# Six projection steps behind each GELU, stores on ScalarE's queue, and operand buffers of the out stage opened at the last projection

## The chip, the cores and the metric

One core of a Trainium2 chip. The metric is the device time in microseconds of one execution. TensorE, VectorE, ScalarE, GpSimd and SyncE stand in the profile as PE, DVE, ACT, POOL and SP; SP and a part of POOL only issue transfers here. Each engine takes its instructions in the order of its own list.

## The reference

One layer over x (2048 x 1024), all in float32: one input projection, eight heads of forgetting attention beside spatial gating on eight groups, a common out projection, then a SwiGLU FFN.

```python
xn = rms_norm(x, mix_norm_g)
q, k, v, f_logit, z = split(xn @ w_in)          # 512, 512, 512, 8, 1024
attn = forgetting_attention(q, k, v, log_sigmoid(f_logit + b_f))
zu, zv = split(gelu(z))                          # exact GELU, 512 each
zv = layer_norm(zv, ln_g, ln_b)
sgu = zu * (einsum('gij,bcjgd->bcigd', masked w_s, zv) + b_s)
merged = concat(rms_norm(attn), rms_norm(sgu))
x = x + merged @ w_out
x = x + (silu(gate) * up) @ w_down               # gate, up from rms_norm(x) @ w_gate_up
return rms_norm(x, final_norm_g)
```

## The kernel before

Matrix products are made of split operands: each float32 operand is rounded to a high part (a cast on ACT, L110) and a low part (the rest, a subtraction on DVE, L113), and high by high, high by low and low by high are summed, so a product is three matmuls. The program runs in four stages: the projection of q, k and v (to 341 us), the attention stage with the z projection and the gating worked in between (to some 1010 us), the out projection (its matmuls, `oz`, L1072, from 928.8 us on), and the FFN (L1509).

The attention stage is a loop of 320 steps (h, j, kb): head, chunk of 512 queries, block of 128 keys. In a step `qk` makes two score matmuls `st` (L674, L675), an exp on ACT (L677, `Pt`), a cast `Ph` (L110, ACT) and the low part `Pl` (L113, DVE). `pv_of` multiplies both by V two steps later (L707, L709, L712). There are two `st` banks. A stream `lm` makes the row maxima ahead (L332 on PE, L334 on DVE). At the end of a (h, j), `fin` copies the row sums (`lv`, L720, ACT), stores one row of them to SD (L721, SP), makes the numerator `nd` (L722) and stores it to AT (L723, SP). When a chunk has all heads, the sums are read back, inverted and stored to RD (L728 to L731).

Into these steps the generator `gates()` weaves the z projection: 256 projection steps of three matmuls (L824), paced by the step number over ZEND = 280 of the 320 steps. `z_proj` takes a group of four 128-token tiles, with operands `xz` loaded by SP; behind its 32 steps stands one GELU over the whole group (L832). There are eight groups, so eight GELUs: four of the v half, each followed by `v_side` (layer norm, mixing), then four of the u half, each followed by `u_side`: product with the mixed gate (L881), squares (L883), scaling (L888), PE transposes (L891), copies `wsth`/`wstl` on ACT (L894) and a store to ST (L895, SP).

The out stage takes per 128-token tile the transposed operands from ST and AT (`out_prep`, L989, L990), multiplies by RD (L993, L997), squares and sums (L1001 to L1015), and splits. At step OPEN = 268 the preparation of tiles 0 and 1 starts in the gating's own buffers. After the last projection and the gating's end, `stz.close()` frees the gating's buffers, and `out_open()` opens the out stage's: `strm` (raw operands and their high and low parts), `xap`, `pev` and the PSUM pool. From the next step on `out_tiles` puts out matmuls between the last attention steps, for tiles 0 and 1 first.

`behind(*newest)` orders an instruction after the newest cast and low part of the attention, so that it does not overtake them. The order of an engine's list otherwise comes from a scheduler that works on what the program states.

Of the kernel before, what the change touches and what calls it, by code (L numbers as in the profile page):

```python
# [58 lines left out]
LEND = 276  # L59
LEAD = 14  # L60
ZF = 3
OPEN = 268
ORATE = 2
FT = 9
ND = 4
# [12 lines left out]
def trunk(ctx: ExitStack, tc: tile.TileContext, x, x_t, mix_g, w_in, b_f, ln_g, ln_b, w_st, b_st, on_g, w_out,  # L78
# [505 lines left out]
    ps2_[0] = ps2  # L584
    stz = st2.enter_context(ExitStack())
    p2z = pool(stz, "p2z", bufs=2)
    p2m = pool(stz, "p2m", bufs=2)
    psz = pool(stz, "psz", bufs=2, space=PSUM)
    wst_h = T(p2z, [P, 8, P], F32R, "wsth", bufs=1)
    wst_l = T(p2z, [P, 8, P], F32R, "wstl", bufs=1)  # L590
# [125 lines left out]
    def fin(h, j):  # L716
        pr, o = h // 2, (h % 2) * DH
        pv, _ = live.pop((h, j))
        nd, lv = T(p2, [DH, CH], F32, "nd", bufs=1), T(p2, [DH, CH], F32, "lv", bufs=1)
        nc.scalar.copy(lv, pv[DH:P])  # L720
        ld(SD[j][h : h + 1], lv[0:1])  # L721
        nc.vector.scalar_tensor_tensor(nd, lv, m0[0:DH], pv[0:DH], ALU.mult, ALU.add)  # L722
        ld(AT[j][o : o + DH, pr, :], nd)  # L723
        heads[j] += 1
        if heads[j] == H:
            yield
            sr = T(p2, [P, H * CH // P], F32, "sr")
            ld(sr, SD[j].rearrange("h (a t) -> (h a) t", t=H * CH // P))  # L728
            yield
            nc.vector.reciprocal(sr, sr)  # L730
            ld(RD[j].rearrange("h (a t) -> (h a) t", t=H * CH // P), sr)  # L731
        yield
# [3 lines left out]
    def z_consts():  # L736
        wsr = T(p2z, [P, 8, P], F32, "zr", bufs=2)
        yield
        ld(wsr, w_st.rearrange("g j i -> j g i"))
        bsc = T(p2z, [P, 8], F32, "bsc", bufs=1)  # L740
        ld(bsc, b_st)
        lngb = T(p2z, [P, 512], F32, "lngb", bufs=1)
        ld(lngb, ln_g.rearrange("(o n) -> o n", o=1).broadcast_to([P, 512]))
        lnbb = T(p2z, [P, 512], F32, "lnbb", bufs=1)
        ld(lnbb, ln_b.rearrange("(o n) -> o n", o=1).broadcast_to([P, 512]))
        ZC.update(bsc=bsc, lngb=lngb, lnbb=lnbb)
        yield
        nc.vector.memset(wsr[64:128, :, 0:64], 0.0)
        hi_of(nc.scalar, wst_h, wsr)
        lo_of(nc.vector, wst_l, wsr, wst_h)  # L750
        yield
# [45 lines left out]
    def at_u(*at):  # L797
        if at == (0, 2, 0):
            ld(onc, on_g.rearrange("(k p) -> p k", p=P))
            wl_[:] = out_part(0)  # L800
            wl_[0](0, raw2)
            wl_[0](1, raw2)
        if at in O_AT:
            n = O_AT.index(at)
            wl_[1](n)
            if n in (1, 3):
                wl_[0](n // 2 + 2, raw2)
        if at[1:] == (3, 4):
            m = mixes[at[0]] = T(p2z, [P, 4, CH], F32, "zvh", bufs=1)
            ld(m, GD[at[0]])  # L810

    def z_proj(q, w, side, extra):

        zr = T(p2z, [P, 4, CH], F32, "zr", bufs=2)
        for cc in range(4):
            t = 4 * q + cc
            xz = T(p2z, [P, 2, KT, P], F32R, "xz")
            for a in range(2):
                ldr(xz[:, a], XS[q][:, a, :, cc * P : (cc + 1) * P])
            pz = T(psz, [P, CH], F32, "z", bufs=NZ)  # L820
            n = 0
            for k in range(KT):
                for a, b in ((0, 0), (0, 1), (1, 0)):
                    nc.tensor.matmul(pz, xz[:, a, k, :], w[b][:, k, :], start=n == 0, stop=n == 3 * KT - 1)  # L824
                    n += 1
                extra(q, cc, k)
                if k % 2:
                    next(side, None)
                yield
            nc.scalar.activation(zr[:, cc, :], pz, AF.Copy, scale=r1[:, t : t + 1])  # L830
        with behind(*newest):
            nc.scalar.activation(zr, zr, AF.Gelu)  # L832
        return zr

    def v_side(q, zr):

        yield
        yield
        mv = T(p2, [P, 4, 2], F32, "mv", bufs=1)
        for cc in range(4):  # L840
            with behind(*newest):
                bs = T(p2, [P, 6], F32, "bs")
                nc.vector.bn_stats(bs, zr[:, cc, :])
                nc.vector.bn_aggr(mv[:, cc, :], bs)
            if cc % 2:
                yield
        rv = rsqrt(p2, mv[:, :, 1], 1.0, "rl", n=4)
        zvh = T(p2z, [P, 8, 4, DH], F32R, "zvh", bufs=1)
        zvl = T(p2z, [P, 8, 4, DH], F32R, "zvl", bufs=1)
        for cc in range(4):  # L850
            with behind(*newest):
                zv = zr[:, cc, :]
                nc.vector.scalar_tensor_tensor(zv, zv, mv[:, cc, 0:1], ZC["lngb"], ALU.subtract, ALU.mult)
                nc.vector.scalar_tensor_tensor(zv, zv, rv[:, cc : cc + 1], ZC["lnbb"], ALU.mult, ALU.add)
                zv8 = zv.rearrange("p (g d) -> p g d", g=8)
                hi_of(nc.scalar, zvh[:, :, cc, :], zv8)
                lo_of(nc.vector, zvl[:, :, cc, :], zv8, zvh[:, :, cc, :])
            yield
        for gg in range(4):
            px = T(psz, [P, 2, 4, DH], F32, "z", bufs=NZ)  # L860
            for g2 in range(2):
                g = gg * 2 + g2
                for n, (a, b) in enumerate(((wst_h, zvh), (wst_h, zvl), (wst_l, zvh))):
                    nc.tensor.matmul(px[:, g2].rearrange("p c d -> p (c d)"), a[:, g, :],
                                     b[:, g].rearrange("p c d -> p (c d)"), start=n == 0, stop=n == 2)
            yield
            for g2 in range(2):
                g = gg * 2 + g2
                nc.vector.tensor_scalar_add(zr[:, :, g * DH : (g + 1) * DH], px[:, g2], ZC["bsc"][:, g : g + 1])
        ld(GD[q], zr)  # L870
        yield

    def u_side(q, zr):

        yield
        yield
        ss = T(p2, [P, 4], F32, "ss2", bufs=1)
        m = mixes.pop(q)
        for cc in range(4):
            with behind(*newest):  # L880
                nc.vector.tensor_tensor(zr[:, cc, :], zr[:, cc, :], m[:, cc, :], ALU.mult)  # L881
                jk = T(p2, [P, CH], F32, "jk", bufs=1)
                nc.scalar.activation(jk, zr[:, cc, :], AF.Square, accum_out=ss[:, cc : cc + 1])  # L883
            yield
        rs = rsqrt(p2, ss, 1.0 / 512, "rs", n=4)
        yield
        for cc in range(4):
            nc.vector.tensor_scalar_mul(zr[:, cc, :], zr[:, cc, :], rs[:, cc : cc + 1])  # L888
            tp = T(psz, [P, 4, P], F32, "z", bufs=NZ)
            for k in range(4):  # L890
                nc.tensor.transpose(tp[:, k, :], zr[:, cc, k * P : (k + 1) * P], ident)  # L891
            yield
            sT = T(p2z, [P, 4, P], F32, ("wsth", "wstl")[cc % 2], bufs=1)
            nc.scalar.copy(sT, tp)  # L894
            ld(ST[4 * q + cc], sT)  # L895


    units = [(h, j) for h in range(H) for j in range(NCH)]
# [2 lines left out]
    def gates():  # L901
        side = iter(())
        for w, extra, then in ((wzv, at_v, v_side), (wzu, at_u, u_side)):
            for q in range(NCH):
                zr = yield from z_proj(q, w, side, extra)
                for _ in side:
                    yield "on"
                side = then(q, zr)
        for _ in side:
            yield  # L910
# [57 lines left out]
            yield  # L968

    def out_open():  # L970
        nonlocal strm, pev, xap
        xap = pool(ctx, "xap", bufs=2, side="right")
        strm = pool(ctx, "strm", side="right")
        pev = evac_pool(0)
        pso = pool(ost, "pso", bufs=2, space=PSUM)
        E["bank"] = lambda: T(pso, [P, CH], F32, "oz")
# [5 lines left out]
    def out_prep(t, o, space=None):  # L982
# [40 lines left out]
        if space is not None:  # L1023
            o["ahead"] = True
            while not strm:
                yield
            inputs()
            low = split(r[:, 4:8, :])
        o["s"] = (split(at), low)
        yield  # L1030

# [74 lines left out]
    zc = z_consts()  # L1106
    next(zc)
    zg = gates()
    z_total = H * 4 * KT
    z_done = o_done = 0  # L1110
    og = wg = None
    fins = []
# [2 lines left out]
    for n in range(len(steps) + DEPTH):  # L1115
# [25 lines left out]
        if z_done == z_total and not wg:  # L1141
            while next(zg) == "on":
                pass
            wg = out_weights()
        if n >= OPEN:
            if not first:
                E["tp"] = lambda: T(ps2, [P, 4, P], F32, "mx_ps", bufs=NMX)
                z = T(p2z, [P, 4, 4, P], F32, "zvl", bufs=1)
                first += [out_prep(t, o[t], (z[:, 2 * t], z[:, 2 * t + 1])) for t in range(2)]
            with behind(*newest):  # L1150
                for g in first:
                    next(g, None)
        if z_done == z_total and not strm:
            if all([next(zg, 0) == 0 for _ in range(ZF)]) and all(o[t].get("ahead") for t in range(2)):
                stz.close()
                out_open()
                o_from = n + 1
        if strm and not og and n > o_from:
            og = out_tiles()
        while og and o_done < (n - o_from) * ORATE:  # L1160
            with behind(*newest):
# [409 lines left out]
```

## Time and profile before

| | us |
|---|---|
| median of 3 runs | 2455.67 |
| lowest, highest | 2453.19, 2455.75 |
| the profiled execution | 2457.9 |
| its span, first to last instruction | 2456.2 |
| PE busy in it | 2386.1 (97%) |
| DVE, ACT, POOL busy | 1664.5, 1054.6, 611.1 |
| mean granted TensorE clock | 0.985 of full |

The shares are means over four stages with different limits. A stretch in which PE stands still, or in which its granted clock is below 1, is found in the table by stretches and in the timelines; a gap of a line is the idle time ahead of it on its own engine, with what ended it.

### The profile page before, as it was taken

To read this page: it belongs to the slowest core of one execution; us is meant where nothing else is said; L and a number is where in the kernel's file an instruction comes from. 1 tells how busy PE (TensorE), PEld (TensorE's weight loads), DVE (VectorE), ACT (ScalarE), POOL (GpSimd) and SP (SyncE) were. 2 spreads that over 40 slices of the span, in tenths; PEclk is the share of its full clock that TensorE was granted. 3 is DMA by queue.
4 is the path that set the end of the run, shared out by engine and by line. 5 is a ranking of instruction groups with operands and counts; after the bars stand their busy time and mean duration, and the time that the engine had idled before them with its cause. 6 is when DMAs were issued, how large, how long until landed. Compare 5 with 4: busy or idle time off the path is not lost. (4 is left out here: it accounts for less than half of the span.)

```text
span 2456.2 us, 31368 instructions
## 1 busy us (share of the span) xinstructions
PE 2386.1 (97%) x10585; PEld 1903.9 (78%) x10585; DVE 1664.5 (68%) x2710; ACT 1054.6 (43%) x1770; POOL 611.1 (25%) x662
## 2 busy tenths in 40 slices
PE   9999999999999988999999999999999999999997
PEld 7778777777777666778888888888888887888886
DVE  6557667888877555555765555875555587696888
ACT  5322137766777664434432323433233242332333
POOL 1000011122111211122232322233223244454441
PEclk9999999999999989999999999999999999999999
DMA  8856466555565656665523223342222335455453
GB/s 283 285 168 202 132 198 180 157 153 164 150 179 160 167 155 196 189 193 170 172 77 103 69 86 86 107 134 69 86 80 84 95 114 187 172 189 192 148 186 144
DMA packets 404919, 372.08 MB, mean 151 GB/s; under 512 B 72660, under 2 KB 326420, under 8 KB 402712
## 3 DMA queue, kind: packets, MB, share of 16 engines
q1 hardware_dynamic: 401880, 359.59, 47.7%
q0 software_dynamic: 2880, 10.49, 1.4%
q8 instruction: 85, 1.39, 0.2%
q14 instruction: 74, 0.61, 0.1%
HBM read 249.09 MB, written 120.92 MB: 151 GB/s over the span
## 5 line engine op out<-in xcount | busy, mean ns | idle before, releaser
L110 ACT CAST wh<-raw 128x512 fp32r<-128x512 f32 (+2 forms) x496 | 304.1, 620 | 756.4 <-PE pp L1509 609.9
L113 DVE TENSOR_TENSOR wl<-raw,wh 128x512 fp32r<-128x512 f32 (+2 forms) x496 | 370.9, 757 | 93.5 <-ACT wh L110 93.2
L1509 PE MATMUL pp<-wl,wh 128*128 128x512 f32 x1056 | 326.5, 390 | 1.7 <-ACT u L1265 1.0
L1509 PE MATMUL pp<-wh,wh 128*128 128x512 f32 x1056 | 326.1, 390 | 0.0
L1199 POOL TENSOR_TENSOR raw<-raw 128x512 f32<-128x512 f32 (+1 forms) x124 | 170.4, 1375 | 507.1 <-DMA raw<-in_w_gu_dram 342.8
L113 DVE TENSOR_TENSOR Pl<-Pt,Ph 128x512 fp32r<-128x512 f32 (+1 forms) x320 | 194.9, 613 | 109.1 <-ACT Ph L110 96.7
L1509 PEld LDWEIGHTS pp<-wl,wh 128*128 128x128 f32 x1056 | 198.0, 188 | 44.7 <-ACT u L1265 1.4
L1509 PEld LDWEIGHTS pp<-wh,wh 128*128 128x128 f32 x1056 | 198.2, 188 | 41.9
L677 ACT ACTIVATE Pt<-st 128x512 f32<-128x512 f32 (+1 forms) x320 | 167.3, 533 | 129.8 <-PE st L675 125.5
L1509 PE MATMUL pp<-wl,wl 128*128 128x512 f32 x528 | 206.2, 391 | 0.7 <-DVE wl L113 0.7
L1509 PE MATMUL pp<-wh,wl 128*128 128x512 f32 x528 | 206.0, 390 | 0.0
L824 PE MATMUL z<-wh,xz 128*128 128x512 f32 x512 | 191.8, 403 | 2.1 <-DMA xz<-XS 2.1
L1199 DVE TENSOR_TENSOR raw<-raw,raw 128x512 f32<-128x512 f32 (+1 forms) x112 | 133.3, 1192 | 79.0 <-POOL raw L1199 75.2
L110 ACT CAST Ph<-Pt 128x512 fp32r<-128x512 f32 (+1 forms) x320 | 175.3, 557 | 26.4 <-PE pv L709 11.3
L334 DVE TENSOR_REDUCE mx<-mx_ps 128x1 f32<-128x512 f32 x192 | 129.4, 684 | 35.5 <-PE mx_ps L332 35.1
L687 POOL TENSOR_SCALAR_AFFINE_SELECT Ph<-Ph 128x128 fp32r<-128x128 f32 x128 | 49.4, 386 | 409.6 <-DVE Pl L113 317.0
L674 PE MATMUL st<-A,D 74*128 74x512 f32 (+1 forms) x320 | 123.9, 387 | 9.2 <-ACT Pt L677 8.9
L707 PE MATMUL pv<-Ph,V 128*128 128x512 f32 (+1 forms) x320 | 122.4, 382 | 10.5 <-POOL Ph L687 6.1
L712 PE MATMUL pv<-Pl,V 128*128 128x512 f32 (+1 forms) x320 | 123.3, 385 | 1.8 <-DVE Pl L113 1.0
L332 PE MATMUL mx_ps<-D,A 66*128 66x512 f32 (+2 forms) x320 | 118.2, 385 | 6.0 <-DMA D<-KH 3.7
L675 PE MATMUL st<-B,C 128*128 128x512 f32 (+1 forms) x320 | 120.4, 376 | 0.0
L1509 PEld LDWEIGHTS pp<-wl,wl 128*128 128x128 f32 x528 | 99.1, 188 | 23.0 <-DVE wl L113 1.6
(315 smaller groups left out, 5300.6 us busy)
## 6 DMA issues: line engine op xcount, KB each, us to landing
raw<-in_w_gu_dram SPq DMA_DIRECT2D x88, 512.0 KB
xz<-XS SPq DMA_DIRECT2D x64, 512.0 KB
HD<-hT SPq DMA_DIRECT2D x44, 512.0 KB
D<-KH SPq DMA_DIRECT2D x112, 128.0 KB
XA<-xa SPq DMA_DIRECT2D x27, 512.0 KB
raw<-HD SPq DMA_DIRECT2D x24, 512.0 KB
XA<-xb SPq DMA_DIRECT2D x21, 512.0 KB
xa<-XA SPq DMA_DIRECT2D x20, 512.0 KB
```

The lines of the kernel that those rows point to most:

```text
L110: return nc.scalar.copy(o, i) if eng is nc.scalar else eng.tensor_copy(o, i)
L113: return eng.tensor_tensor(o, i, f(h), ALU.subtract)
L332: nc.tensor.matmul(pm[:, 0:n], lhs, Dt[0 : lhs.shape[0], 0:n], start=True, stop=True)
L334: nc.vector.tensor_reduce(mx[:, a, s : s + 1], pm, AX.X, ALU.max)
L674: nc.tensor.matmul(st[:, off:], Dt[:, b * P : (b + 1) * P], A[:, off:], start=True, stop=False)
L675: nc.tensor.matmul(st[:, off:], C[:, b * P : (b + 1) * P], B[:, off:], start=False, stop=True)
L677: nc.scalar.activation(Pt[:, off:], st[:, off:], AF.Exp)
L707: nc.tensor.matmul(pv[:, off:], V[:, 0:P], Ph[:, off:], start=kb == 0, stop=False)
L712: nc.tensor.matmul(pv[:, off:], V[:, 0:P], Pl[:, off:], start=False, stop=kb == 4 * j + 3)
L824: nc.tensor.matmul(pz, xz[:, a, k, :], w[b][:, k, :], start=n == 0, stop=n == 3 * KT - 1)
L1199: (nc.vector if e == "v" else nc.gpsimd).tensor_tensor(o, a, b, op)
L1509: nc.tensor.matmul(pm, a[:, k, :], b[:, k, :], start=on is None and k == 0 and e == 0, stop=k == it.kh - 1 and e == 2, skip_group_check=n ...
```

## The change

It has three parts. First, `z_proj` gets a number `burst`: for the first six projection steps of a group it yields "on", which makes the loop go on at once, so with the step that follows seven projection steps stand in a row at the beginning of a group, that is behind the GELU of the group before. The first group has none. The pace of the others is spread over 42 steps fewer. Second, the stores of row sums to SD and of transposed tiles to ST are issued by ACT. Third, some of the gating's buffers (`lngb`, `lnbb`, `xz`, `zvl` and those of the row maxima) lie in a pool set `sty` of their own, which is closed at the last projection; `strm` takes its place there, so the second half of w_out and the low parts of tiles 0 and 1 are made before the gating has ended. The row maxima and the preparation of tiles 0 and 1 are driven to their ends at that point. `stz.close()` and `out_open()` wait for the gating alone. OPEN becomes 265, and from the second group of u on the mixed gate is loaded at another step.

```diff
-OPEN = 268
+OPEN = 265
+BURST = 6
...
-    p2m = pool(stz, "p2m", bufs=2)
+    sty = st2.enter_context(ExitStack())
+    p2y = pool(sty, "p2y", bufs=2)
+    p2m = pool(sty, "p2m", bufs=2)
...
-        ld(SD[j][h : h + 1], lv[0:1])
+        nc.scalar.dma_start(SD[j][h : h + 1], lv[0:1])
...
-        if at[1:] == (3, 4):
+        if at[1:] == ((2, 0) if at[0] else (3, 4)):
             m = mixes[at[0]] = T(p2z, [P, 4, CH], F32, "zvh", bufs=1)
             ld(m, GD[at[0]])
...
-    def z_proj(q, w, side, extra):
+    def z_proj(q, w, side, extra, burst):
...
-                yield
+                yield "on" if cc == 0 and k < burst else None
...
-            ld(ST[4 * q + cc], sT)
+            nc.scalar.dma_start(ST[4 * q + cc], sT)
...
-                zr = yield from z_proj(q, w, side, extra)
+                zr = yield from z_proj(q, w, side, extra, 0 if q == 0 and then is v_side else BURST)
...
     def out_open():
-        nonlocal strm, pev, xap
+        nonlocal pev, xap
         xap = pool(ctx, "xap", bufs=2, side="right")
-        strm = pool(ctx, "strm", side="right")
...
             while not strm:
                 yield
+            low = split(r[:, 4:8, :])
+            o["s"] = (split(at), low)
+            while not xap:
+                yield
             inputs()
-            low = split(r[:, 4:8, :])
+            yield
+            return
...
-    z_total = H * 4 * KT
+    z_total = H * 4 * KT - 7 * BURST
...
         if z_done == z_total and not wg:
             while next(zg) == "on":
                 pass
+            for _ in lm:
+                pass
+            while not all(o[t].get("ahead") for t in range(2)):
+                for g in first:
+                    next(g)
+            sty.close()
+            strm = pool(ctx, "strm", side="right")
             wg = out_weights()
...
-        if z_done == z_total and not strm:
-            if all([next(zg, 0) == 0 for _ in range(ZF)]) and all(o[t].get("ahead") for t in range(2)):
+        if wg and not xap:
+            if all([next(zg, 0) == 0 for _ in range(ZF)]):
                 stz.close()
                 out_open()
                 o_from = n + 1
-        if strm and not og and n > o_from:
+        if xap and not og and n > o_from:
             og = out_tiles()
```

PE at the sixth GELU (755.1 us in the trace), before, from the score pair on whose exp is the first behind the GELU; line numbers and tile numbers differ a little between the two programs:

```order
L674 MATMUL st_8363<-A_8070,D_858_3356 128x512
L675 MATMUL st_8363<-B_8073,C_853_3351 128x512
L707 MATMUL pv_8181<-Ph_8314,V_847_3338 128x256
L709 MATMUL pv_8181<-Ph_8314,V_847_3338 1x256
L712 MATMUL pv_8181<-Pl_8316,V_847_3338 128x256
L674 MATMUL st_8380<-A_8070,D_858_3356 128x512
L675 MATMUL st_8380<-B_8073,C_853_3351 128x512
L332 MATMUL mx_ps_8389<-D_8109,A_7620 128x512
L707 MATMUL pv_8181<-Ph_8332,V_847_3338 128x128
L709 MATMUL pv_8181<-Ph_8332,V_847_3338 1x128
L712 MATMUL pv_8181<-Pl_8334,V_847_3338 128x128
L674 MATMUL st_8399<-A_8070,D_858_3356 128x512
```

The same place in the changed program, from the score pair whose exp is the last ahead of the GELU:

```order
L677 MATMUL st_8356<-A_8078,D_858_3359 128x512
L678 MATMUL st_8356<-B_8081,C_853_3354 128x512
L827 MATMUL z_8373<-wh_3233,xz_8370 128x512
L827 MATMUL z_8373<-wl_3234,xz_8370 128x512
L827 MATMUL z_8373<-wh_3233,xz_8370 128x512 x2
L827 MATMUL z_8373<-wl_3234,xz_8370 128x512
L827 MATMUL z_8373<-wh_3233,xz_8370 128x512 x2
L827 MATMUL z_8373<-wl_3234,xz_8370 128x512
```

Before, PE has one more score pair and small PV matmuls there. Now the projection of the next group follows, 21 matmuls in a row, of which the first are shown.

ACT at the eighth GELU, before:

```order
L830 ACTIVATE zr_9160<-z_9764,r_2_64 128x512
L677 ACTIVATE Pt_10128<-st_10125 128x512
L832 ACT_TABLE_LOAD
L832 ACTIVATE zr_9160<-zr_9160 128x2048
L110 CAST Ph_10130<-Pt_10128 128x512
L677 ACT_TABLE_LOAD
L677 ACTIVATE Pt_10155<-st_10152 128x512
L883 ACTIVATE jk_9926,ss_2673_9924<-zr_9160 128x512
```

And now, with what each instruction waits for (`DMAHW0` to `DMAHW7` are the eight landing semaphores that transfers of SP and ACT take in turn; the other names are engines):

```order
L723 COPY lv_9903<-pv_9606 64x512 [waits DMAHW1_49,PE_49]
L680 ACTIVATE Pt_9892<-st_9889 128x512 [waits PE_49]
L724 DMA SD_110_173<-lv_9903 1x512 [waits DMAHW0_49,Activation_49]
L111 CAST Ph_9894<-Pt_9892 128x512 [waits Activation_49,Pool_49]
L680 ACTIVATE Pt_9913<-st_9910 128x512 [waits DVE_49,PE_49]
L833 ACTIVATE zr_9163<-z_9748,r_2_64 128x512 [waits PE_49]
L111 CAST Ph_9915<-Pt_9913 128x512 [waits DVE_49,Activation_49]
L835 ACT_TABLE_LOAD
L835 ACTIVATE zr_9163<-zr_9163 128x2048 [waits Activation_49]
L111 CAST wh_9932<-raw_9637 128x512 [waits DMAHW3_49,DMAHW2_49]
L111 CAST wh_9936<-raw_9637 128x512 [waits DMAHW7_49,DMAHW1_49]
L111 CAST wh_9940<-raw_9642 128x512
```

Now a store to SD stands between an exp and a cast, and waits for a landing semaphore too; casts of the out operands (`wh<-raw`) follow the GELU, four in all, ahead of the next exp.

SP at the opening of the out stage, before (`raw_10112` is the operand tile of token tile 2):

```order
L895 DMA ST_98_161<-wsth_10010 128x512
L107 DMA V_848_3339<-VD_77_140 128x4x1
L895 DMA ST_99_162<-wstl_10019 128x512
L107 DMA C_856_3354<-KH_3_58_121 64x512
L107 DMA C_856_3354<-KL_3_74_137 64x512
L721 DMA SD_111_174<-lv_10339 1x512
L978 DMA ffb_10049<-in_ffn_g_dram 128x1024
L989 DMA raw_2727_10099<-ST_87_150 128x512
L990 DMA raw_2727_10099<-AT_100_163 128x4x128
L993 DMA rd_10100<-RD_112_175 64x4x128 x2
L989 DMA raw_10112<-ST_86_149 128x512
L990 DMA raw_10112<-AT_100_163 128x4x128
```

And now, where that tile is `raw_10128`:

```order
L991 DMA raw_2732_10128<-ST_86_149 128x512
L992 DMA raw_2732_10128<-AT_100_163 128x4x128
L108 DMA C_856_3357<-KL_3_74_137 64x512
L108 DMA D_861_3362<-AUG_146 10x4x128
L991 DMA raw_2823_10500<-ST_88_151 128x512
L992 DMA raw_2823_10500<-AT_101_164 128x4x128
L980 DMA ffb_10079<-in_ffn_g_dram 128x1024
L1010 DMA xa_10096<-in_x_dram 128x1024
L1010 DMA xa_10098<-in_x_dram 128x1024
L995 DMA rd_10116<-RD_112_175 64x4x128 x2
L995 DMA rd_10129<-RD_112_175 64x4x128 x2
```

The loads of tile 2 stood behind two of the last four stores to ST, a store to SD and the loads of tile 3; now no store is ahead of them here, and the loads of x and RD come behind.

## Rows read from the trace of the kernel before

**Rows 1.** The page, busy time, share of the span and instructions of each engine.

```profile
PE 2386.1 (97%) x10585; PEld 1903.9 (78%) x10585; DVE 1664.5 (68%) x2710; ACT 1054.6 (43%) x1770; POOL 611.1 (25%) x662
```

**Rows 2.** Stretches: from:to, length, PE, PEld, DVE, ACT, POOL busy (instructions), clock, DMA share, GB/s.

```profile
480.00:490.00 10.00, 10.00 (x44) 7.38 (x43) 6.83 (x12) 9.87 (x14) 0.00 (x0) 1.00 0.38 96
...
555.00:558.40 3.40, 3.18 (x8) 2.30 (x9) 1.27 (x3) 3.37 (x6) 0.00 (x0) 0.50 0.27 93
...
691.50:698.30 6.80, 6.20 (x15) 4.85 (x16) 3.22 (x5) 3.17 (x6) 0.00 (x0) 0.50 0.61 149
...
759.80:766.60 6.80, 6.35 (x15) 4.85 (x16) 4.80 (x8) 4.73 (x9) 0.00 (x0) 0.50 0.19 43
...
831.50:834.90 3.40, 3.40 (x10) 1.98 (x11) 2.18 (x4) 3.35 (x8) 0.54 (x2) 0.50 1.00 279
...
910.00:920.20 10.20, 8.36 (x27) 5.32 (x25) 6.66 (x14) 7.84 (x19) 2.66 (x7) 0.50 0.00 0
...
944.10:954.40 10.30, 5.18 (x14) 4.08 (x15) 8.08 (x14) 2.66 (x5) 2.23 (x3) 0.50 0.61 159
440.00:480.00 40.00, 39.13 (x192) 30.94 (x191) 33.62 (x67) 26.15 (x49) 7.87 (x16) 1.00 0.63 177
```

**Rows 3.** Timeline of ACT at the sixth GELU: start, duration, engine, line, operation.

```profile
755.08 1.28 ACT L832 ACT_TABLE_LOAD   x1
756.38 1.91 ACT L832 ACTIVATE zr<-zr 128x2048 f32<-128x2048 f32 x1
758.30 1.28 ACT L677 ACT_TABLE_LOAD   x1
```

**Rows 4.** Timeline of PE at the sixth GELU; in brackets idle time before, and its releaser.

```profile
755.77 0.40 PE L674 MATMUL st<-A,D 74*128 74x512 f32 x1
756.01 0.40 PE L675 MATMUL st<-B,C 128*128 128x512 f32 x1
...
760.25 0.80 PE L674 MATMUL st<-A,D 74*128 74x512 f32 x1 [3.38 <-ACT Pt L677]
760.84 0.63 PE L675 MATMUL st<-B,C 128*128 128x512 f32 x1
761.26 0.63 PE L674 MATMUL st<-A,D 74*128 74x512 f32 x1
```

**Rows 5.** Timelines of PE at the third, fifth and seventh GELU.

```profile
555.22 0.80 PE L707 MATMUL pv<-Ph,V 128*128 128x512 f32 x1 [0.58 <-ACT Ph L110]
...
692.10 0.80 PE L674 MATMUL st<-A,D 74*128 74x512 f32 x1 [1.79 <-ACT Pt L677]
...
828.65 1.10 PE L332 MATMUL mx_ps<-D,A 66*128 66x512 f32 x2 [0.55 <-DVE mx L334]
831.38 0.61 PE L674 MATMUL st<-A,D 74*128 74x384 f32 x1 [1.63 <-ACT Pt L677]
```

**Rows 6.** Timeline of PE behind the eighth GELU.

```profile
909.55 0.50 PE L707 MATMUL pv<-Ph,V 128*128 128x512 f32 x1 [3.14 <-DMA D<-KH]
...
911.46 0.69 PE L674 MATMUL st<-A,D 74*128 74x384 f32 x1 [0.61 <-ACT Pt L677]
...
915.89 0.79 PE L707 MATMUL pv<-Ph,V 128*128 128x512 f32 x1 [1.22 <-POOL Ph L687]
```

**Rows 7.** Timelines of PE and ACT at the opening of the out stage.

```profile
949.22 0.58 PE L1015 MATMUL mx_ps<-ones_c,sq 128*128 128x1 f32 x2 [8.85 <-POOL sq L1004]
...
943.66 0.62 ACT L110 CAST wh<-raw 128x512 fp32r<-128x512 f32 x1 [9.70 <-DMA raw<-ST]
```

**Rows 8.** SP's waits (total, times, longest), ST stores (ns min/median/max), landing of POOL's loads (us).

```profile
SPq L721 <- ACT lv L720: 41.8, 18, 7.6
SPq L107 <- DVE mr L351: 34.7, 9, 9.1
...
L895 SPq DMA_DIRECT2D ST<-wsth x8: 319/332/1633, 726.7 to 923.4; - x8
...
raw<-in_w_out_dram POOLq DMA_DIRECT2D x6, 512.0 KB, 5.3
```

More of the change, by code (lines that the diff above doesn't have):

```diff
@@ L741, in z_consts @@
         ld(bsc, b_st)
-        lngb = T(p2z, [P, 512], F32, "lngb", bufs=1)
+        lngb = T(p2y, [P, 512], F32, "lngb", bufs=1)
         ld(lngb, ln_g.rearrange("(o n) -> o n", o=1).broadcast_to([P, 512]))
-        lnbb = T(p2z, [P, 512], F32, "lnbb", bufs=1)
+        lnbb = T(p2y, [P, 512], F32, "lnbb", bufs=1)
         ld(lnbb, ln_b.rearrange("(o n) -> o n", o=1).broadcast_to([P, 512]))
@@ L816, in z_proj @@
             t = 4 * q + cc
-            xz = T(p2z, [P, 2, KT, P], F32R, "xz")
+            xz = T(p2y, [P, 2, KT, P], F32R, "xz")
             for a in range(2):
@@ L848, in v_side @@
         zvh = T(p2z, [P, 8, 4, DH], F32R, "zvh", bufs=1)
-        zvl = T(p2z, [P, 8, 4, DH], F32R, "zvl", bufs=1)
+        zvl = T(p2y, [P, 8, 4, DH], F32R, "zvl", bufs=1)
         for cc in range(4):
@@ L1147, in trunk @@
                 E["tp"] = lambda: T(ps2, [P, 4, P], F32, "mx_ps", bufs=NMX)
-                z = T(p2z, [P, 4, 4, P], F32, "zvl", bufs=1)
+                z = T(p2y, [P, 4, 4, P], F32, "zvl", bufs=1)
                 first += [out_prep(t, o[t], (z[:, 2 * t], z[:, 2 * t + 1])) for t in range(2)]
```

## The prediction

> **What bounds the kernel now.** I read the page first: TensorE is busy 2386.1 of 2456.2 us [rows 1], so time can come only from the places where it stands still or runs at half clock. The table by stretches of the attention stage [rows 2] shows where: most stretches look like 440 to 480 us, with PE busy 39.13 of 40 us at full clock and VectorE 33.62, but there are short stretches at a granted clock of 0.50, the lower level of 1.2 GHz. Four of them stand right behind GELUs (the third, fifth, sixth and seventh of eight), one behind the eighth, and one at the opening of the out stage. The timelines tell why. ScalarE's GELU is 1.28 + 1.91 + 1.28 us of table load, activation and table load back [rows 3], and no exp is made in these 4.5 us. PE works off what it has behind the last score pair, then waits for the next exp: 3.38 us at the sixth GELU [rows 4], 0.58, 1.79 and 0.55 + 1.63 us at the third, fifth and seventh [rows 5]. At the second nothing is lost, as the stretch from 480 to 490 us shows [rows 2]; the first and the fourth are alike.
>
> **The bursts.** The idle time at these four GELUs is 0.58 + 1.79 + 3.38 + 2.18 = 7.9 us. Behind each the clock falls: 3.4, 6.8, 6.8 and 3.4 us at 0.50 [rows 2]. Full matmuls start 0.42 us apart there, against 0.24 us just before [rows 4], so about half of such a stretch is lost: 20.4 / 2 = 10.2 us. Together 18.1 us, the most that the bursts can give back at GELUs 1 to 7. Seven projection steps are 21 matmuls, 21 x 0.24 = 5.0 us of PE work that waits for no exp. At the sixth GELU PE lacked 3.4 us; the order puts 21 of them in a row behind the last score pair, and at the other six places it is the same kind of row. The work is only moved: 42 steps fewer are spread between the GELUs, 42 x 3 x 0.24 = 30 us over some 560 us. VectorE, busy 84% there [rows 2], then has up to 5% less time per attention step, which it still has. I take **-17 us**, a little under the whole, since exps may come late in other places; the ends are 0 and -18.1.
>
> The Trainium skill (ScalarE: Activation LUTs, section What ACT_TABLE_LOAD costs) speaks against this cover: it puts a switch of tables at about 2.66 us, a load of some 1.28 us and a drain of some 1.38 us. By that a GELU would hold the exps up about 7.2 us (an estimate from that page), 2.8 more, and a burst would leave gaps at the GELUs that have little else behind them. In the trace the activation starts 1.30 us after the load, and the load back 1.92 us after the activation [rows 3]: no drain shows, and the sum goes by the rows.
>
> **The eighth GELU** has no burst. PE idles 3.14 + 0.61 + 1.22 us there [rows 6], and 10.2 us are at half clock [rows 2]. In the new order four casts of out operands and one square stand between GELU and the load back, where one cast stood: about four more ScalarE instructions of the size of the cast at 943.66 us, 0.62 us [rows 7], so 2.5 us. PE has about 2 us more behind its last score pair than before, counted from its rows at 0.24 us a full matmul. Ends: 0 and +2.5 for the wait, and up to half of a further 3.4 us at low clock. I take **+3 us**.
>
> **The opening of the out stage.** PE stands 8.85 us at the sum of squares of token tile 2 and then runs 949.2 to 954.4 us at half clock, 5.2 / 2 = 2.6 us: 11.4 us [rows 7, 2]. ScalarE had waited 9.70 us for the load from ST [rows 7], so the chain is load, product, square, two GpSimd adds, PE, behind 48 out matmuls that PE does in a row with nothing else. In the new order of SyncE these loads stand ahead of the x tiles and the RD loads, no longer behind ST and SD stores, and score and PV matmuls stand between the out matmuls. The chain, some 9 us, then runs under that work. I take **-10 us**, most of 11.4; ends 0 (the chain is as late again, since RD of this chunk or ScalarE is late) and -11.4.
>
> **The stores on ScalarE's queue.** 32 stores of row sums and 16 of transposed tiles leave SyncE and go between exps. The issue itself was 0.33 us for an ST store on SyncE [rows 8]; 48 x 0.33 = 16 us of ScalarE time, in a stage where it is busy 26.15 of 40 us [rows 2]: nothing on the path. What the stores may wait for costs more. Each DMA takes one of eight landing semaphores in turn, and 46 of the 48 wait until the transfer that had it before, mostly one of SyncE's eight places back, has landed. ScalarE is in order, so the casts and exps behind a store wait as well, then the score matmuls. The trace of before has no such wait. Lower end: all those transfers have long landed, 0. Upper end for one store: the transfer's own landing, 5.3 us for 512 KB in the nearest row, or that SyncE has not issued it yet since it stands in a wait itself, up to 9.1 us for VectorE [rows 8]. SyncE waits a good part of this stage, and I estimate that a third of the stores, 15, find such a transfer open, for 2.5 us on average, 38 us of ScalarE. What that costs PE is read from the GELUs: eight times 4.5 us without an exp gave 7.9 + 5.0 = 12.9 us idle, a share of 0.36, but a short stall stays under PE's stock of work more often. I take half of 0.36 x 38: **+6 us**. On the other side SyncE no longer stands 41.8 us in 18 waits for the row-sum copies [rows 8], so its key loads come earlier; PE hardly waited for them, and I give nothing for it.
>
> **The rest.** The preparation of tiles 0 and 1 is driven to its end in one piece at the last projection, with its SD store, row-sum load, reciprocal, RD store and loads, while projection operands stand behind it on SyncE: 0 to +8 (about the chain of 8.85 us of tile 2, without its cover); I take **+3 us**. The second half of w_out loads earlier on GpSimd's queue and costs nothing new. The load of the mixed gate at step (2,0) instead of (3,4) is one SyncE issue, covered by its use a GELU later.
>
> **Sum:** -17 + 3 - 10 + 6 + 3 = -15 us against the profiled execution's 2457.9 us, so 2442.9; the median of the runs is 2455.67, 2.2 lower, so **2441 us**.
>
> **Rivals.**
> - *ScalarE waits for SyncE's transfers* (the other side). It decides when the stalls cost PE more than the 21 us that the other terms give. With 20 stores held 4.5 us, 90 us, at the full share of 0.36 it is 32 us: -21 + 32 = +11, about 2467 us. For it: nearly every store has such a wait, and SyncE's waits of up to 9.1 us sit ahead of the transfers. Against: a landing semaphore comes round only after seven other transfers, and PE holds one or two steps of work. Chance 0.18.
> - *The gain is given back.* The bursts fill the GELUs, but score work behind a burst comes in a lump on ScalarE and VectorE, and thinner projection work between leaves PE waiting at other steps: a quarter of the 17 us stays. Then -4 + 3 - 10 + 6 + 3 = -2, about 2454 us. For it: VectorE at 84%. Against: the mean leaves room. Chance 0.13.
> - *Everything is covered.* No stall, no late preparation: -18 + 3 - 11.4 = -26, about 2429 us. For it: each wait has a cover that can be named. Chance 0.13.
> - That the bursts are not where they are meant to be is excluded by the order of PE's rows. By the drain that the Trainium skill states (above) the bursts would give some 12 us instead of 17; the rows do not bear it out, and it lies inside the range of my forecast.
>
> **How the numbers follow.** The forecast, 2441 us with its own range of 2432 to 2449, has 0.56. A measurement here tells a change from none by about 0.2%, 4.9 us: faster is below 2450.8, slower above 2460.6. Faster: 0.56 + 0.13 + a quarter of 0.13 = 0.72. Slower: 0.16 of the 0.18. The same: the other 0.10 and 0.02, 0.12. The range goes from 2426, which leaves out half of the full cover, to 2464, which leaves out a good half of the slower case.
>
> **What would show it.** In the new profile: PE without a gap over 0.5 us at GELUs 1 to 7 and full clock behind them; at the eighth a gap of 5 us or more; no gap of 8 us at the sum of squares of tile 2; ScalarE's waits for transfers ahead of its stores, some 40 us in all, and PE's waits for exp outside the GELUs up by about 6 us. The forecast is wrong if ScalarE's waits there reach 90 us, if half-clock stretches stay behind bursts, or if PE stands more than 8 us in the preparation of tiles 0 and 1.

## The result and the profile after

The changed kernel takes 2425.8 us (median of 4 runs, 2422.36 to 2428.99) against 2454.43 us for the kernel before (4 runs): ratio 0.9884, 95% interval 0.9864 to 0.9904. That is 28.6 us, where 14.7 were forecast, and 0.2 us under the range. Faster was right. The size was not, and the experiments show that the reason was not either: the gain is that of the stores, to which the forecast had given a loss. One execution of the kernel before (11206.76 us) and one of opening_only (8016.91 us) were in a slow state and are left out of all numbers.

The page of the changed kernel, busy time, and the line of its one core with the mean clock; below them the same line for the kernel before:

```profile
PE 2369.9 (98%) x10585; PEld 1902.6 (78%) x10585; DVE 1667.1 (69%) x2710; ACT 1059.1 (44%) x1770; POOL 610.3 (25%) x662
```

```profile
core 0: 2427.1 us, clock 0.989
```

```profile
core 0: 2456.2 us, clock 0.985
```

Two numbers can be made of such lines, and they are used for every run below: idle is span minus PE's busy time, and clock loss is span times (1 - clock). Before they were 70.1 and 36.8 us, now 57.2 and 26.7 us; the clock is given to 0.001, so clock loss is known to about 1.2 us. So 12.9 us of idle time and 10.1 us of clock loss are gone, of a span that is 29.1 us shorter; the rest lies in PE's busy time, whose matmuls include short waits.

At the sixth GELU, where PE had stood 3.38 us [rows 4], the timeline of ScalarE and that of PE now read (start, duration, engine, line, operation):

```profile
745.78 1.28 ACT L835 ACT_TABLE_LOAD   x1
747.07 1.92 ACT L835 ACTIVATE zr<-zr 128x2048 f32<-128x2048 f32 x1
...
750.49 1.28 ACT L680 ACT_TABLE_LOAD   x1
751.78 1.08 ACT L680 ACTIVATE Pt<-st 128x512 f32<-128x512 f32 x2
```

```profile
744.02 0.40 PE L678 MATMUL st<-B,C 128*128 128x512 f32 x1
744.25 0.39 PE L827 MATMUL z<-wh,xz 128*128 128x512 f32 x1
...
748.91 0.40 PE L827 MATMUL z<-wh,xz 128*128 128x512 f32 x1
749.15 0.27 PE L710 MATMUL pv<-Ph,V 128*128 128x256 f32 x1
...
752.43 0.50 PE L677 MATMUL st<-A,D 74*128 74x512 f32 x1
```

ScalarE is without an exp even longer than before, from 745.78 to 751.78 us, for a square stands ahead of the load back. PE spends 744.25 to 749.15 us on the 21 projection matmuls, and no idle time is marked at the score pair behind them. By the table by stretches the clock stays up there, as it does at the third, fifth and seventh GELU. It falls behind the eighth GELU and at the opening, and also, where it had not fallen before, from 406 and from 857 us on (columns as in [rows 2]):

```profile
745.00:756.00 11.00, 10.86 (x50) 8.46 (x49) 5.51 (x13) 9.80 (x14) 0.00 (x0) 1.00 0.74 190
...
406.00:410.00 4.00, 4.00 (x12) 3.02 (x12) 0.80 (x2) 1.21 (x2) 0.72 (x1) 0.57 0.58 165
...
857.00:864.00 7.00, 6.97 (x21) 5.50 (x22) 3.65 (x7) 1.04 (x3) 4.54 (x9) 0.52 0.00 0
...
877.40:887.70 10.30, 6.08 (x13) 3.90 (x14) 8.28 (x14) 10.27 (x23) 0.72 (x1) 0.50 0.52 144
...
915.00:921.80 6.80, 6.43 (x18) 5.08 (x19) 3.70 (x7) 3.09 (x6) 0.84 (x2) 0.50 0.71 190
```

The gaps in front of these stretches, from PE's timeline, and what ScalarE did at the eighth GELU. The first two are waits for the projection's operands `xz`, of which PE has 7.2 us in all here and had 2.1 before:

```profile
405.78 0.50 PE L827 MATMUL z<-wh,xz 128*128 128x512 f32 x1 [2.89 <-DMA xz<-XS]
...
855.43 0.47 PE L827 MATMUL z<-wh,xz 128*128 128x512 f32 x1 [1.35 <-DMA xz<-XS]
```

```profile
881.62 0.80 PE L677 MATMUL st<-A,D 74*128 74x512 f32 x1 [6.54 <-ACT Pt L680]
```

```profile
915.17 0.59 PE L1017 MATMUL mx_ps<-ones_c,sq 128*128 128x1 f32 x2 [3.28 <-POOL sq L1006]
```

```profile
875.05 1.91 ACT L835 ACTIVATE zr<-zr 128x2048 f32<-128x2048 f32 x1
876.87 2.16 ACT L111 CAST wh<-raw 128x512 fp32r<-128x512 f32 x4
878.94 0.62 ACT L886 ACTIVATE jk<-zr 128x512 f32<-128x512 f32 x1
```

The four casts and the square stand ahead of the exp, as the order said, and PE waits 6.54 us where it waited 4.97 in three pieces [rows 6]. The chain of tile 2 ends 3.28 us late instead of 8.85 [rows 7].

Last, the waits. Of ScalarE's waits from 341 to 1010 us, these are all that end with a transfer among those that the profile lists (total, times, longest):

```profile
ACT wh L111 <- DMA raw<-ST: 2.3, 1, 2.3
...
ACT wsth L897 <- DMA md<-mr: 0.6, 1, 0.6
...
ACT wstl L897 <- DMA ST<-wstl: 0.3, 1, 0.3
ACT wsth L897 <- DMA ST<-wsth: 0.3, 1, 0.3
```

The forecast had 38 us here. SyncE's waits for the row-sum copies, 41.8 us [rows 8], are gone, and with them most of another, that for the maxima of `md`, which had been 34.7 us:

```profile
SPq L108 <- DVE mr L352: 13.8, 8, 4.7
```

SyncE does not stand less for it: its listed waits in this time add up to 318 us before and 333 now. It waits longer at the store that comes next, that of the numerator `nd`, which is worked out from the same copy `lv`. Before, and now:

```profile
SPq L723 <- DVE nd L722: 17.4, 16, 3.1
```

```profile
SPq L726 <- DVE nd L725: 42.0, 18, 5.5
```

### The profile page after: what moved, and what is told of

Read it like the earlier page. It is cut to its first block, busy times and chain, and to the rows that moved or that the text cites. A ratio compares the mean times of both kernels' runs of the same rounds, so it can differ in the third digit from the quotient of the medians.

```text
span 2427.1 us, 31390 instructions
## 1 busy us (share of the span) xinstructions
PE 2369.9 (98%) x10585; PEld 1902.6 (78%) x10585; DVE 1667.1 (69%) x2710; ACT 1059.1 (44%) x1770; POOL 610.3 (25%) x662
## 5 line engine op out<-in xcount | busy, mean ns | idle before, releaser
L827 PE MATMUL z<-wh,xz 128*128 128x512 f32 x512 | 197.8, 404 | 7.2 <-DMA xz<-XS 7.2
L827 PEld LDWEIGHTS z<-wh,xz 128*128 128x128 f32 x512 | 97.7, 192 | 30.0 <-DMA xz<-XS 8.3
```

## The experiments

After the result there were two theories. A: the bursts gave back the GELUs' gaps, the opening the rest, and the stores cost nothing. B: the stores on ScalarE's queue are the gain, since SyncE no longer stands at them with the loads of other work behind it. The first four runs take the three parts apart.

All runs together; idle and clock loss are worked out as above, each from the run's own page. A page is of one execution: the slowest of its run for no_store_move, the change, change_again and change_late_casts, the fastest for sd_stores_only, so a few us between two pages say little. The ratio is to the kernel before, run beside it (2451.76, 2452.64 and 2453.0 us in the three groups of four).

| run | bursts | stores on | early buffers | us | ratio, interval | idle | clock loss |
|---|---|---|---|---|---|---|---|
| before | no | SyncE | no | 2451.76 to 2454.43 | 1 | 70.1 | 36.8 |
| bursts_only | yes | SyncE | no | 2445.41 | 0.9974, 0.9962 to 0.9987 | 67.4 | 31.8 |
| opening_only | no | SyncE | yes | 2447.8 | 0.9981, 0.9969 to 0.9993 | 67.9 | 24.4 |
| no_store_move | yes | SyncE | yes | 2448.02 | 0.9988, 0.9978 to 0.9998 | 69.1 | 34.3 |
| stores_only | no | ScalarE | no | 2420.57 | 0.9876, 0.9863 to 0.9889 | 53.5 | 21.8 |
| stores_opening | no | ScalarE | yes | 2419.86 | 0.9866, 0.9851 to 0.9881 | 51.8 | 19.3 |
| stores_bursts | yes | ScalarE | no | 2417.22 | 0.9856, 0.9839 to 0.9872 | 52.7 | 16.9 |
| the change | yes | ScalarE | yes | 2425.8 | 0.9884, 0.9864 to 0.9904 | 57.2 | 26.7 |
| change_again | yes | ScalarE | yes | 2420.15 | 0.987, 0.9857 to 0.9883 | 55.9 | 24.2 |
| change_late_casts | yes | ScalarE | yes | 2416.74 | 0.9853, 0.984 to 0.9866 | 52.8 | 26.6 |
| sd_stores_only | no | SD on ScalarE | no | 2422.45 | 0.9875, 0.9858 to 0.9892 | 55.3 | 16.9 |
| st_stores_only | no | ST on ScalarE | no | 2444.56 | 0.996, 0.9945 to 0.9976 | 64.3 | 31.8 |
| stores_on_gpsimd | no | GpSimd | no | 2424.71 | 0.9884, 0.9869 to 0.9899 | 55.8 | 19.4 |
| sd_store_doubled | no | ScalarE, SD also on SyncE | no | 2442.68 | 0.9957, 0.9944 to 0.997 | 66.4 | 29.3 |

### One part alone, and the change without the stores

**bursts_only** is the kernel before with `burst` in `z_proj`, BURST = 6 and `z_total` as in the diff above.

> The kernel before, with the bursts alone. Theory A (the bursts give back what GELUs 3, 5, 6 and 7 lost, 7.9 us of idle time and half of 20.4 us at half clock, and the rest of the gain is the opening): 18 us less than before, about 2436 us, no PE gap over 0.6 us and full clock behind GELUs 1 to 7, the 8.85 us gap at the sum of squares of tile 2 still there. Theory B (the parts only work together: SyncE's waits hold the operands of the bursts): a gain of at most 9 us, 2445 us or more, with PE waiting for xz in the bursts.

**stores_only**:

```diff
-        ld(SD[j][h : h + 1], lv[0:1])
+        nc.scalar.dma_start(SD[j][h : h + 1], lv[0:1])
...
-            ld(ST[4 * q + cc], sT)
+            nc.scalar.dma_start(ST[4 * q + cc], sT)
```

> The kernel before, with the 48 stores on ScalarE's queue alone. Theory A (the stores neither cost nor gain): within 3 us of before. The prediction's term: 6 us slower, 2460 us, ScalarE waiting some 40 us at the stores. Theory B (SyncE, freed of its 45 us of waits for the row-sum copies, loads earlier and PE gains small waits all over the stage): 6 to 10 us faster, about 2447 us.

**opening_only** is the changed kernel with BURST = 0 and the two lines above the other way round.

> The changed kernel without bursts and with the stores back on SyncE: the early operand buffers alone. Theory A: 8 to 11 us faster than before, about 2445 us, with the gap at the sum of squares of tile 2 down from 8.85 to about 3 us and the gap at GELU 8 up to about 6.5 us. Theory B (the early buffers need the stores off SyncE, since the loads of tile 2 else stand behind ST stores): less than 4 us faster, the gap at tile 2 still 7 us or more.

**no_store_move** is the changed kernel with those two lines alone the other way round.

> The changed kernel with the 48 stores back on SyncE. Theory A (the stores neither cost nor gain): the changed kernel's time, 2423 to 2429 us. The prediction's term (stores cost 6 us): 2420 us. Theory B (the move gains by freeing SyncE): 2433 us or more, with more PE waits for key and projection loads.

Measured: 6.4, 31.2, 4.0 and 3.7 us faster than before. Theory A falls with each of them: it gave bursts_only 18 us and the change without the store move the change's own time. Theory B's 6 to 10 us for the stores was also far too little. Without the bursts and without the early buffers, the stores alone give 31 us, as much as the whole change. The early buffers alone do at the opening what was expected, the gap at tile 2 is 1.61 us there, where theory B had expected 7 or more, but PE idles 6.55 us behind the casts at GELU 8.

Why the bursts alone do so little is seen at their sixth GELU. PE's and ScalarE's timelines, and SyncE's issues in the same time, of bursts_only:

```profile
747.31 0.40 PE L708 MATMUL pv<-Ph,V 128*128 128x512 f32 x1
747.78 0.50 PE L713 MATMUL pv<-Pl,V 128*128 128x512 f32 x1
752.18 0.80 PE L675 MATMUL st<-A,D 74*128 74x512 f32 x1 [3.90 <-ACT Pt L678]
```

```profile
747.02 1.28 ACT L833 ACT_TABLE_LOAD   x1
```

```profile
747.53 1.02 SPq L108 DMA_DIRECT2D xz<-XS  x2
754.38 0.24 SPq L722 DMA_DIRECT2D SD<-lv  x1
...
757.08 1.01 SPq L108 DMA_DIRECT2D xz<-XS  x2
```

The projection's operands for this burst are issued from 747.53 us on, half a microsecond after the GELU's table load began, and PE is dry at 748.28. There was nothing to burst with, and PE's list has no projection there. Then SyncE stands from 748.55 to 754.38 us at a row-sum store, with the next `xz` behind it. In the changed kernel two such loads were issued 7.75 us ahead of the burst that begins at 744.25 us:

```profile
736.50 1.06 SPq L108 DMA_DIRECT2D xz<-XS  x2
...
745.71 1.01 SPq L108 DMA_DIRECT2D xz<-XS  x2
```

In the kernel before, the first two loads come earlier, 3.4 us ahead of the sixth GELU (755.08 us, PE dry at 756.87), but PE's list has its first projection behind the GELU only at 765.11 us. SyncE's timeline and that matmul:

```profile
751.72 2.21 SPq L107 DMA_DIRECT2D xz<-XS  x2
...
757.20 0.44 SPq L107 DMA_DIRECT2D A<-md  x1
762.84 0.22 SPq L721 DMA_DIRECT2D SD<-lv  x1
...
765.30 1.02 SPq L107 DMA_DIRECT2D xz<-XS  x2
```

```profile
765.11 0.63 PE L824 MATMUL z<-wh,xz 128*128 128x512 f32 x1
```

The store waits 5.2 us from 757.64 on, since the copy `lv` that it stores stands behind the GELU on ScalarE. The next pair of `xz` stands behind it and waits as well, though it has nothing to do with the row sums. And in stores_only, without any burst, projection matmuls stand in PE's list over the whole GELU, whose table load begins at 735.74 us:

```profile
735.09 0.40 PE L824 MATMUL z<-wh,xz 128*128 128x512 f32 x1
...
736.77 0.40 PE L824 MATMUL z<-wh,xz 128*128 128x512 f32 x1
...
738.53 0.40 PE L824 MATMUL z<-wh,xz 128*128 128x512 f32 x1
...
740.92 0.51 PE L674 MATMUL st<-A,D 74*128 74x512 f32 x1 [0.31 <-ACT Pt L677]
```

3.38 us of idle time have become 0.31.

### Two parts at a time, one kind of store, another queue

**stores_bursts** is the kernel before with both of the edits of bursts_only and stores_only; **stores_opening** is the changed kernel with BURST = 0.

> Stores on ScalarE's queue and bursts, without the early buffers of the out stage. Theory B (SyncE's waits at the stores held the projection operands; with the stores gone the projection stands behind the GELUs anyway, so bursts add nothing): the time of the stores alone, 2418 to 2424 us. The prediction's sum (opening worth 10 us): 2436 us. A third way: the bursts cost something once the gaps are gone, by lumps of score work or of xz loads behind them: 2424 to 2430 us, with PE waiting for xz.

> The changed kernel without bursts. Theory B: no gap over 1 us at GELUs 1 to 7 all the same, and 2417 to 2426 us. The prediction's sum (bursts worth 17 us): 2443 us, with gaps of 1.8 to 3.4 us at GELUs 5 to 7. If the opening gives what it was given, it is 8 to 10 us below the stores alone, 2411 us; if the casts ahead of the exp at GELU 8 eat that, it is within 4 us of 2420.

Measured: 2417.22 and 2419.86 us. Against the stores alone the bursts give another 3.4 us and the early buffers 0.7, less than the intervals can tell. In the whole change the bursts show no gain: without them it takes 2419.86 us, with them 2425.8 and 2420.15. The forecast's 17 us for the bursts are not there to be had a second time: without bursts the projection stands at the GELUs too, if its operands are there.

**sd_stores_only** has only the first of the two edits of stores_only.

> The kernel before, with the 32 row-sum stores alone on ScalarE's queue; the 16 ST stores stay on SyncE. In its order the projection stands behind GELUs 3, 5 and 6 and not behind 7. Theory B, read from the gaps of before at these three (5.75 us idle, half of 17.0 us at half clock): 14 us faster than before, about 2437 us, with a gap of some 2 us left at GELU 7. If instead the ST stores carry it, under 5 us faster.

**stores_on_gpsimd** has `nc.gpsimd.dma_start` in both places.

> The kernel before, with the 48 stores on GpSimd's queue instead of ScalarE's. Theory B (what counts is that SyncE no longer stands at them): within 5 us of the stores on ScalarE, 2420 to 2426 us, no gap at GELUs 3, 5, 6 and 7. Rival (it is ScalarE's queue that matters, which issues right behind its own copy, or GpSimd's masks come late behind stores that wait): 2435 us or more, PE waiting for GpSimd's masks.

Measured: 2422.45 and 2424.71 us. The 32 row-sum stores of 2 KB each carry the gain, 30 us, twice what was read from the gaps at three GELUs; a gap of 2.32 us is left at the seventh, as expected. From 341 to 800 us PE idles 8.2 us in this run where it idled 17.9 before, and the clock is 1.00 there where it was 0.97. The gaps at the three GELUs were 5.75 us of these, so small waits elsewhere went as well. That GpSimd's queue does as well as ScalarE's shows in the second run. GpSimd now stands at these stores longer than SyncE did:

```profile
POOL SD L721 <- ACT lv L720: 77.9, 26, 7.0
```

Yet the masks that stand behind come only a little late; of PE's waits from 341 to 1010 us this is their share:

```profile
PE pv L707 <- POOL Ph L687: 2.9, 4, 1.3
```

### The wait put back

**sd_store_doubled** is stores_only with a second store of each row of sums on SyncE, to a DRAM tensor that nobody reads.

```diff
+    S2 = [T(dram, [H, CH], F32, f"SX{c}") for c in range(NCH)]
...
-        ld(SD[j][h : h + 1], lv[0:1])
+        nc.scalar.dma_start(SD[j][h : h + 1], lv[0:1])
+        ld(S2[j][h : h + 1], lv[0:1])
```

> The kernel with all 48 stores on ScalarE's queue, and a second copy of each of the 32 row-sum stores put back on SyncE, to a DRAM tensor that nobody reads. Theory B (the cost is that SyncE stands at these stores until ScalarE has copied, with the loads behind them): most of the gain is gone, 2440 to 2452 us, gaps at GELUs 6 and 7 again and SyncE waiting some 40 us for ScalarE's copies. Rival (ScalarE's queue gains by itself, by earlier row sums): stays at 2420 to 2425 us.

Measured: 2442.68 us, 10.3 us faster than the kernel before, where stores_only was 31.2. About 21 us are lost again by 32 transfers of 2 KB that nobody reads. SyncE's waits and PE's gap at the seventh GELU (at the sixth, where one was expected too, the longest is 0.70 us):

```profile
SPq L723 <- ACT lv L721: 44.5, 22, 5.8
```

```profile
818.65 0.69 PE L675 MATMUL st<-A,D 74*128 74x384 f32 x1 [2.61 <-ACT Pt L678]
```

The rival, that earlier row sums by ScalarE's queue are the gain, had them here as well, and falls. Not ruled out is that part of the loss comes from the added transfers themselves: 12.8 us of SyncE's waits here are for the landing of a row-sum store, against 2.0 in stores_only.

But theory B is right only in part, for SyncE is not freed. Its listed waits from 341 to 1010 us add up to 318 us before, 320 in sd_stores_only and 331 here. In sd_stores_only it stands at the store of `nd` almost as long as at both stores before (41.8 + 17.4 us):

```profile
SPq L723 <- DVE nd L722: 57.6, 25, 9.7
```

What differs is which loads stand ahead of that wait. In stores_only, behind its sixth GELU, they are `xz` and V:

```profile
739.70 0.39 SPq L107 DMA_DIRECT2D xz<-XS  x1
740.13 1.68 SPq L107 DMA_DIRECT2D V<-VD  x3
744.33 0.47 SPq L723 DMA_DIRECT2D AT<-nd  x1
```

An estimate for all eight groups, from the timelines: with 24 projection matmuls counted to each pair of `xz` loads, in order, the second load of a pair is issued 6.8 to 7.9 us on average ahead of the first of these matmuls in the six kernels with the row-sum stores on SyncE (6.9 with the doubled stores), and 9.5 to 17.5 us in those without. That goes with the times; that it makes all of the difference is not shown.

**st_stores_only** has only the second edit of stores_only.

> The kernel before with the 16 ST stores alone on ScalarE's queue. Theory B, narrowed (the row-sum stores carry it): 2 to 9 us faster than before, 2444 to 2450 us, the gaps at GELUs 5 to 7 still there and that at GELU 8 gone, where its order has projection behind it. If either kind of store frees SyncE alike, 2425 us or less.

Measured: 2444.56 us, 8.4 us faster than before, and close to the run with the doubled stores, which also has ST on ScalarE and SyncE standing at the row sums. The time is that of theory B as narrowed, the gaps are not: at the eighth GELU, where none was expected, PE waits 3.57 us for an exp and later 3.43 for a cast.

### The casts at the eighth GELU

**change_late_casts** is the changed kernel with two more steps in `out_prep`:

```diff
+DLY = 2
...
             while not strm:
                 yield
+            for _ in range(DLY):
+                yield
             low = split(r[:, 4:8, :])
```

> The changed kernel, with the four casts of the out operands of tiles 0 and 1 two steps later, so that one exp stands behind GELU 8 as in the kernel before. If the casts at GELU 8 are what the early buffers cost (gap 6.5 us against 3.7 us, and 3.4 us more at half clock), the time falls by about 5 us to the stores and bursts alone, 2416 to 2420 us, or lower, to 2412, if the opening's gap (3.3 us against 8.4 in two pieces) then counts too. If the cost is elsewhere (xz waiting at the bursts), it stays at 2423 to 2429 us.

**change_again** is the changed kernel, beside it.

> The changed kernel once more beside the others, to compare with stores and bursts alone on one chip: 2422 to 2429 us. If the 8 us between the two were the chip's, it comes within 3 us of 2417.

Measured: 2416.74 and 2420.15 us. The casts do leave the GELU: PE's gap there is 3.84 us in the profile of change_late_casts, against 6.54. But the times differ by 3.4 us, the intervals overlap, and the executions of the changed kernel lie from 2419.5 to 2429.0 us over both groups. So a gain from the later casts is possible and not shown, and up to 5.7 us of the 8.6 between the change and stores_bursts were not the kernels'. One difference is the kernels', and no run takes it apart: PE waits 7.2 us for `xz` in the change, 6.1 in change_again, 4.6 in change_late_casts and 1.3 in stores_bursts. The fastest versions, stores_bursts and change_late_casts at 2417 us, both lie below the change, and clearly below the kernel before; against change_again their intervals don't settle it.

## Why the prediction was right and wrong

**The reading of the gaps held.** PE was lost at four GELUs, at the eighth and at the opening, and half-clock stretches came behind those gaps. Where these gaps went, the stretches went. But the gaps that were priced, 7.9 + 5.0 + 8.85 us, are 21.8 of the 70.1 us of idle time, and the stretches some 20 of the 36.8 us of clock loss; the stores alone gave more than the 18 us that the four GELUs held. The table doesn't show idle and clock loss falling together everywhere: opening_only has 2.2 us less idle time than before and 12.4 less clock loss.

**The store term failed.** "I take half of 0.36 x 38: **+6 us**" was -31 us for the stores alone (and half of 0.36 x 38 is 6.8). Two things were wrong in it. ScalarE's waits, put at 38 us, came to 3.5 us among those listed, so the lower of the two bounds was near. And the other side of the move was dismissed: "its key loads come earlier; PE hardly waited for them, and I give nothing for it". That the move is worth 30 us is shown, by sd_stores_only, stores_on_gpsimd and sd_store_doubled. The way from there to PE is in part argued: PE's waits hardly name the loads, 2.1 us for `xz` before, since its list has other work where the projection could stand, and it then idles at an exp. The 41.8 us of SyncE's waits [rows 8] were the row to follow: what stands behind the store on SyncE, and which matmul needs it. Behind it stood `xz`, the operand of the very work that was to fill the GELU.

**The burst term** was -17; alone the bursts gave 6.4 us, on top of the stores 3.4. The gaps were sized well, but the cover was credited to the wrong edit. The 21 matmuls behind each GELU were read from the order of the whole change; with the bursts alone no projection stands behind the sixth. In the change the first sign held only in part: PE waits 0.96 us for `xz` behind the first GELU and 0.76 behind the seventh.

**The opening's three terms** (+3 at the eighth GELU, -10 at the opening, +3 for the preparation, together -4) gave 4.0 us alone. That they meet is luck, for the parts do not. In the change the eighth GELU cost 1.6 us more (6.54 us idle for 4.97, the half-clock stretch as long as before). The opening gave not 10 but 4.8 us: 3.28 us idle for 8.85, but 6.8 us at half clock for the 5.2 that were counted. The preparation fits best to the stretch from 855 to 864 us, 1.65 us of waits for `xz` and 7 us at half clock, some 5 us for the 3; that this is its doing no run shows.

**The chances.** "Everything is covered", 2429 us, was the nearest case, and was given 0.13, for a reason that is only half of it: next to no stall on ScalarE was right, but that the move itself gains was in no case, and so the range ended 0.2 us above the result.

**The drain** that the Trainium skill (ScalarE: Activation LUTs, section What ACT_TABLE_LOAD costs) states does not show in the changed kernel either: the activation starts 1.29 us after the start of the load, the exp 1.29 us after that of the load back. On the stores, the Trainium skill (DMA: Bandwidth & Descriptors, section Issuing engines are not separate DMA queues) says that issuing from several engines only saves the time of the issue, usually small. The issues here were 32 times some 0.24 us, 8 us of SyncE, and the move gave 30 us. By the runs above the rest goes with the waits ahead of the issues and the loads behind them, of which that section says nothing.

**Left open:** whether the order of PE's list or the late loads themselves cost more. Both change with the place of the store, and no run holds one and changes the other.

## What to carry to other kernels

A store that waits for a busy engine is not cheap because it is small: here 2 KB stores held up the loads behind them on SyncE's list, and that showed as idle time of PE under another name. The queue's total waiting says little, for it hardly changed; what counts is which loads stand behind the wait. Before filling a gap with more work, look when that work's operands are issued, and what the issuing queue waits for just ahead of them. When a change has several parts, read the order of each part alone before giving one of them the gain.

## What was not expected of the hardware

Forty-eight stores on ScalarE's queue cost it next to nothing: 0.22 us of issue for a row-sum store and, of the waits that end with a transfer, 1.2 us in all apart from that for an operand load, though 46 of the stores had a wait for another transfer's landing in the program. In stores_only such waits came to 7.2 us, and it was no slower. GpSimd stood 77.9 us at the row-sum stores, and the kernel was some 4 us from the one with ScalarE.
